# Twelve products instead of six in a step of the dense stream beside the RWKV units

## The chip, the cores and the metric

The kernel runs on one NeuronCore of a Trainium2 chip. The metric is device time in microseconds (us) of one execution. The kernel before took 1853.83 us, the median of 3 runs (1851.74 to 1856.85).

## What is computed

One inference step of a bidirectional hybrid trunk with two layers, float32 in and out, on 128 context tokens and 256 latent tokens (384 columns in all). Layer 0 mixes with a Mamba-2 state-space group (SSD) and an RWKV-7 group side by side, layer 1 with GLA and mLSTM; each layer ends with a squared-ReLU MLP. The change is in layer 0:

```python
def mixer_ab(h, s_ssd, s_rwkv, grid_rows, p):
    proj = h @ p['w_in']
    ssd_in, rw_in = proj[..., :IN_SSD], proj[..., IN_SSD:]
    xbc = silu(short_conv(ssd_in[..., D_SSD:...], ...))
    ...
    rw = rw_in + p['rwkv_mu'] * (token_shift(rw_in) - rw_in)
    ...
    for d in range(2):
        y, s = rwkv7_scan(rh, lw_h[:, :, d], kd, vh, kk, a_h[:, :, d], ...)
    ...
    out = jnp.concatenate([y_ssd, y_rw], axis=-1) @ p['w_out']
```

The RWKV scan runs in chunks of 64 tokens: in each chunk a 64x64 triangular matrix is inverted by doubling, and a state is carried from chunk to chunk.

## The kernel before

Products of the dense projections are split in two for precision: the activations and the weights each have a high and a low half (`h3H`, `h3L`, `wH`, `wL`), and one product of 128 input rows by 128 output columns is three matmuls of 128x384 into one accumulator (`dps`): H by wH, L by wH, H by wL (lines 746 to 749). One output tile has eight such products, 24 matmuls. Weights come in panels of two products; `take` (line 152) has each panel split into wH (ScalarE, line 714) and wL (VectorE, line 715) three panels ahead.

Layer 0 is written as streams of Python generators. `ab_streams` (line 1527) goes through 19 stages; stage s has up to six streams: `chain` (the state recurrence of RWKV unit s-2: `pr`, `pu`, `pd`, `py`), `inv` (the inverse of unit s-1: rounds of `pz`, then `pw2` and `pt2`), `prep0`/`prep1` (operands of unit s), `tail` (norm and gate of a finished head pair: `pm`, `pm2`, `pg`), `ssd1` to `ssd3` (`aux`), and `fill` (the dense products of coming units, of SSD and, in the last stages, of the output projection, with products `mod` for the modulation between them). `run` (line 1584) always steps the stream that is least far along, by the number of steps done over the number expected: `self.steps` holds the numbers, first those written by hand in lines 1533 and 1534, and after a stream has run the number that it had; `PACE` (line 34) scales them. A framework then sets each engine's order from this one, by priority, taking a later instruction where an earlier one isn't ready by its own reckoning.

A step of `fill` is what `dense_cm` (line 728) issues between two `yield`s. Before the change that is a panel, two products (six matmuls), then one step of deferred evacuation work (`step_late`, line 798), then the `yield`:

```python
if self.grain and k % self.grain == self.grain - 1:
    self.step_late()
    yield
```

`self.grain` is 2 (line 2056); `k` counts in the panel. After the last product the accumulator is evacuated and there is one more `yield`. Deferred work is the rest of an evacuation: the SSD convolution (`conv`, line 1006: nine instructions on `cacc` in three parts, then a SiLU) and the token shift of an RWKV column (two instructions, lines 1094 and 1095). In layer 1, `grain` is 2 as well (line 2513). In stages 0 to 15 the dense products have one accumulator bank (`one_acc`), so a new output tile starts when the one before it has been evacuated.

Of the kernel before, what the change touches and what calls it, by code (L numbers as in the profile page):

```python
# [175 lines left out]
class Net:  # L176
# [551 lines left out]
    def dense_cm(self, W, c0, xs, evac, placed=None, blocks=None, ncol=128, width=T, acc=None):  # L728

        if blocks is None:
            n = self.wcfg["nk"] * 128 // ncol
            blocks = [(k, n) for k in range(0, len(xs), n)]

        def steps(dn):
            ps = (self.dacc() if acc is None else acc)[:ncol, :width]
            left = sum(n for _, n in blocks)
            first = acc is None  # L740
            for i, (k0, n) in enumerate(blocks):
                h, lo = dn.take(i)
                for k in range(n):
                    xh, xl = xs[k0 + k]
                    left -= 1
                    self.mm(ps, h[:, k, :], xh, start=first, stop=False)
                    first = False
                    self.mm(ps, h[:, k, :], xl, start=False, stop=False)
                    self.mm(ps, lo[:, k, :], xh, start=False, stop=left == 0 and evac is not None)
                    if self.grain and k % self.grain == self.grain - 1:  # L750
                        self.step_late()
                        yield
            more = evac(ps) if evac is not None else None
            if more is not None and next(more, self) is not self:
                self.late.append(more)
            yield
        return Dense(self, [(W, k0, n, c0, ncol, placed) for k0, n in blocks], steps)
# [769 lines left out]
    def ab_streams(self):  # L1527

        NB = 16
        sh, us, fills = self.sh, self.us, self.fills  # L1530
        st = [dict() for _ in range(NB)]
        py = {}
        self.steps.update({"set": 7, "fill0": 37, "fill1": 24, "fill2": 15, "fill3": 14, "fill14": 16, "fill15": 32, "fill16": 30,
                           "fill17": 29, "ssd1": 11, "ssd2": 6, "ssd3": 9, "prep0": 12, "prep1": 9, "inv": 17, "tail": 3})
        for s in range(NB + 3):
            self.one_acc = s < NB
            self.lpool = LPOOL.get(s, 0)
            if s == 1:

                row = lambda: self.mpool.tile([128, T], F32, tag="nt", name="prow", bufs=2)[:, 0:128]  # L1540
                self.params_tr(self.params_in(range(3, self.params.shape[1] // 128), row, self.nc.sync))
            streams = []
            b = s - 2
            if 0 <= b < NB:
                j, d = divmod(b, 2)
                if d == 0:
                    py[j] = self.psy.tile([128, 512], F32, tag="y", name="py")
                streams.append(("chain", self.rw_chain(j, d, st[b], py[j], sh[j])))
            b = s - 1
            if 0 <= b < NB:  # L1550
                streams.append(("inv", self.seq(self.rw_tokmajor(b % 2, sh[b // 2], st[b]), self.rw_inverse(b % 2, st[b]))))
            b = s
            if b < NB:
                j, d = divmod(b, 2)
                prep = self.rw_prep(j, d, sh[j], st[b])
                if d == 0:
                    streams.append(("prep0", self.seq(self.rw_shared(j, sh[j]), prep)))
                else:
                    streams.append(("prep1", self.seq(prep, self.rw_bonus(j, sh[j]))))
            if s >= 4 and s % 2 == 0 and (s - 4) // 2 < 8:  # L1560
                j = (s - 4) // 2
                streams.insert(0, ("tail", self.rw_tail(j, sh[j], sh[j]["y"])))
            q, g = s % 4, s // 4
            if s < NB and q:
                if q == 1:
                    core = self.ssd_core(g, us[g])
                streams.append(("ssd%d" % q, self.part(core, SSD_PARTS[q])))
            if s == 0:
                streams.append(("set", self.set))
            if fills[s]:  # L1570
                streams.append(("fill%d" % (q if 0 < s < NB - 2 else s), self.pipe(fills[s])))
            self.run(streams)
        return sh[7]["y"]
# [384 lines left out]
    def mixer_ab(self):  # L1958
# [94 lines left out]
        self.AOb, (self.Zb, self.AHb, self.ALb) = bd[:2], bd[2:]  # L2053
        self.rpp = self.pool("rwp", es=eb)
        self.yss = self.sumsq()
        self.grain = 2
        self.drain(self.pipe(self.first[0:4] + [self.flush_late()]))
        self.rw_low()
        self.drain(self.pipe(self.first[4:] + [self.flush_late()]))
# [520 lines left out]
```

## Time and profile before

| | |
|---|---|
| profiled execution, its own time | 1853.32 us |
| its span, first to last instruction | 1851.2 us |
| median of 3 runs | 1853.83 us |
| TensorE (PE) busy | 1765.5 us, 95% of the span |
| VectorE (DVE) busy | 1301.8 us, 70% |
| ScalarE (ACT) busy | 1069.6 us, 58% |
| GpSimd (POOL) busy | 216.6 us, 12% |
| mean granted TensorE clock | 0.98 |

Stages of the program in the span: to 87 us layer 0's norm and first products; 87 to 846 us the streams of `ab_streams`; 846 to 1152 us the MLP of layer 0; 1152 to 1582 us layer 1's mixer; then its MLP. "Busy" is time with an instruction under way. Matmuls overlap: a row's duration is longer than the distance to the next row's start, and it is the distance from start to start that the engine's time is made of. PEclk of 1.00 is the 2.4 GHz level, 0.50 the 1.2 GHz level.

### The profile page before, as it was taken

The page shows a single profiled execution, that of the slowest core. Times are in us where ns is not written, and L with a number is a line of the kernel's source. Part 1 is how long each engine was busy: PE and PEld are TensorE (multiplying, and loading weights), DVE is VectorE, ACT ScalarE, POOL GpSimd, SP SyncE. Part 2 cuts the span into 40 slices and gives each one's busy share as a digit, 9 for nine tenths or more (in the row PEclk, how much of TensorE's full clock was granted, in tenths as well). Part 3 has the DMA queues.
Part 4 walks back from the last instruction along what each step waited for, and adds up shares of the span by engine and source line. Part 5 has one row for each costly group of instructions (what it writes and reads, how often), then busy time and mean ns, then how long its engine had stood idle before and what let it go on. Part 6 is the DMA issues. An engine that isn't in the chain of part 4 may idle for free.

```text
span 1851.2 us, 37384 instructions
## 1 busy us (share of the span) xinstructions
PE 1765.5 (95%) x13661; PEld 1480.9 (80%) x13661; DVE 1301.8 (70%) x2992; ACT 1069.6 (58%) x2688; POOL 216.6 (12%) x270
## 2 busy tenths in 40 slices
PE   7879999999999999999999999899999998999998
PEld 3667767766666677786999998889989897999887
DVE  3698788777878889758766334786786958766434
ACT  3567475746574777646655333777676756755322
POOL 3222111110112011101000000020211212000000
PEclk9889999999999999999999999999999998999999
DMA  8332443333334322345445643333333233344432
GB/s 280 112 88 65 123 133 97 106 87 112 102 105 126 101 65 81 100 119 175 117 124 171 177 146 101 102 91 102 102 94 92 74 108 106 115 125 126 150 134 80
DMA packets 314107, 213.55 MB, mean 115 GB/s; under 512 B 39648, under 2 KB 297494, under 8 KB 313924
## 3 DMA queue, kind: packets, MB, share of 16 engines
q1 hardware_dynamic: 308756, 208.35, 38.6%
q10 hardware_dynamic: 4816, 2.69, 0.5%
q8 instruction: 107, 1.75, 0.4%
q14 instruction: 76, 0.62, 0.1%
q0 software_dynamic: 352, 0.13, 0.0%
HBM read 201.32 MB, written 9.78 MB: 114 GB/s over the span
## 4 chain that ended last, share of the span: by engine, by line
PE 75%; DVE 10%; ACT 8%; DMA 4%; issue 2%; POOL 1%; SPq 0%; DVEq 0%; ACTq 0%; POOLq 0%
PE dps L221 45%; PE o L221 7%; PE ps L221 4%; PE mod L221 3%; PE aux L221 2%; DVE wL L235 2%; PE psc L221 2%; DMA raw<-in_w_mod 2%; PE py L221 1%; PE pt L221 1%; DVE cacc L242 1%; PE pr L221 1%; ACT wH L277 1%; PE pw L221 1%; ACT Zb L277 1%
## 5 line engine op out<-in xcount | busy, mean ns | idle before, releaser
L277 ACT ACTIVATE wH<-raw 128x256 fp32r<-128x256 f32 (+1 forms) x790 | 363.3, 480 | 429.3 <-PE dps L221 309.6
L235 DVE TENSOR_TENSOR wL<-raw,wH 128x256 fp32r<-128x256 f32 (+2 forms) x771 | 398.9, 536 | 243.2 <-ACT wH L277 239.5
L277 ACT ACTIVATE Zb<-pz 64x384 f16<-64x384 f32 x160 | 77.2, 483 | 36.4 <-PE pz L221 34.1
L242 DVE SCALAR_TENSOR_TENSOR cacc<-rows,params,cacc 128x384 f32<-128x384 f32 (+1 forms) x192 | 94.2, 491 | 0.7
L221 PE MATMUL dps<-sH,wH 128*128 128x384 f32 x232 | 85.8, 371 | 4.0 <-DVE m L235 3.5
L221 PE MATMUL dps<-sL,wH 128*128 128x384 f32 x232 | 80.5, 347 | 0.3 <-DVE sL L235 0.2
L221 PE MATMUL dps<-sH,wL 128*128 128x384 f32 x232 | 79.7, 345 | 0.5 <-DVE wL L235 0.5
L221 PE MATMUL dps<-h0H,wH 128*128 128x384 f32 (+1 forms) x147 | 58.9, 401 | 8.2 <-ACT h0H L277 3.5
L235 DVE TENSOR_TENSOR AO<-AHb,rwmask 128x768 f16<-128x768 f16 (+1 forms) x112 | 60.1, 537 | 7.7 <-PE pz L221 6.0
L235 POOL TENSOR_TENSOR BK<-BK,kkk 128x768 f32<-128x768 f32 x16 | 33.8, 2110 | 221.5 <-DVE BK L239 150.5
L221 PE MATMUL mod<-xT,cond 128*32 128x384 f32 (+1 forms) x320 | 55.2, 485 | 3.8 <-DVE Q L235 2.5
L221 PE MATMUL dps<-h6H,wH 128*128 128x384 f32 (+2 forms) x147 | 54.9, 373 | 2.7 <-ACT wH L277 2.7
L221 PE MATMUL dps<-h2H,wH 128*128 128x384 f32 (+1 forms) x147 | 55.6, 378 | 1.4 <-ACT wH L277 1.4
L221 PE MATMUL dps<-h4H,wH 128*128 128x384 f32 (+1 forms) x147 | 54.9, 378 | 2.1 <-ACT h4H L245 2.1
L235 POOL TENSOR_TENSOR gDb<-gb 128x384 f32<-128x384 f32 x28 | 33.2, 1187 | 173.5 <-DVE gb L2230 73.2
L221 PE MATMUL dps<-h1H,wH 128*128 128x384 f32 (+1 forms) x147 | 52.0, 354 | 0.0
L221 PE MATMUL dps<-h6H,wL 128*128 128x384 f32 (+2 forms) x147 | 50.8, 346 | 1.2 <-DVE wL L235 1.2
L221 PE MATMUL dps<-h0H,wL 128*128 128x384 f32 (+1 forms) x147 | 51.7, 351 | 0.0
L221 PE MATMUL dps<-h1H,wL 128*128 128x384 f32 (+1 forms) x147 | 51.6, 351 | 0.0
L221 PE MATMUL dps<-h0L,wH 128*128 128x384 f32 (+1 forms) x147 | 51.5, 356 | 0.0
L221 PE MATMUL dps<-h1L,wH 128*128 128x384 f32 (+1 forms) x147 | 51.3, 355 | 0.0
L221 PE MATMUL dps<-h2H,wL 128*128 128x384 f32 (+1 forms) x147 | 51.1, 348 | 0.0
(1163 smaller groups left out, 5450.0 us busy)
## 6 DMA issues: line engine op xcount, KB each, us to landing
raw<-in_w_mlp_up SPq DMA_DIRECT2D x64, 512.0 KB
raw<-in_w_mlp_down SPq DMA_DIRECT2D x64, 512.0 KB
raw<-in_w_in_ab SPq DMA_DIRECT2D x204, 128.0 KB
xT<-in_w_mod SPq DMA_DIRECT2D x128, 192.0 KB
raw<-in_w_in_cd SPq DMA_DIRECT2D x192, 128.0 KB
raw<-in_w_mod SPq DMA_DIRECT2D x64, 192.0 KB
raw<-in_w_mod SPq DMA_DIRECT2D x32, 256.0 KB
raw<-in_w_out_cd SPq DMA_DIRECT2D x64, 128.0 KB
```

Source lines behind the costliest of these rows:

```text
L221: self.nc.tensor.matmul(out, lhsT, rhs, start=start, stop=stop)
L235: return (eng or self.nc.vector).tensor_tensor(out=out, in0=a, in1=b, op=op)
L242: self.nc.vector.scalar_tensor_tensor(out=out, in0=a, scalar=s, in1=b, op0=op0, op1=op1)
L277: self.nc.scalar.activation(out=out, in_=in_, func=AF.Copy)
```

## The change

`dense_cm` counts products over the whole output tile (`done`) instead of in the panel, and `grain` is 4 in layer 0: a step holds four products, twelve matmuls, and after them two steps of deferred work. An output tile of eight products has two such steps and the evacuation's instead of four and the evacuation's. A tile whose products aren't a multiple of four ends its last step with the last product. The numbers of steps written by hand for the first use of each stream are set anew. In layer 1 `grain` stays 2, and there too each step now calls `step_late` twice.

```diff
         def steps(dn):
             ps = (self.dacc() if acc is None else acc)[:ncol, :width]
             left = sum(n for _, n in blocks)
+            done = 0
             first = acc is None
...
                     self.mm(ps, lo[:, k, :], xh, start=False, stop=left == 0 and evac is not None)
-                    if self.grain and k % self.grain == self.grain - 1:
+                    done += 1
+                    if self.grain and (done % self.grain == 0 or left == 0):
+                        self.step_late()
                         self.step_late()
                         yield
...
-        self.steps.update({"set": 7, "fill0": 37, "fill1": 24, "fill2": 15, "fill3": 14, "fill14": 16, "fill15": 32, "fill16": 30,
-                           "fill17": 29, "ssd1": 11, "ssd2": 6, "ssd3": 9, "prep0": 12, "prep1": 9, "inv": 17, "tail": 3})
+        self.steps.update({"set": 7, "fill0": 18, "fill1": 11, "fill2": 14, "fill3": 16, "fill14": 12, "fill15": 24, "fill16": 22,
+                           "fill17": 34, "ssd1": 11, "ssd2": 6, "ssd3": 9, "prep0": 12, "prep1": 9, "inv": 17, "tail": 3})
...
-        self.grain = 2
+        self.grain = 4
```

What this does to the order of the instructions is seen in the built programs. TensorE in the middle of stage 8, from the last matmul of an inverse round on (`pt_6632` and `pt_6661` are `pt2` of that round; `pu` is the chain's, `dps` the dense products). Before:

```order
L221 MATMUL pt_6632<-Zb,W 64x64
L221 MATMUL dps<-h4H,wH 128x384
L221 MATMUL dps<-h4L,wH 128x384
L221 MATMUL dps<-h4H,wL 128x384
L221 MATMUL dps<-h5H,wH 128x384
L221 MATMUL dps<-h5L,wH 128x384
L221 MATMUL dps<-h5H,wL 128x384
L221 MATMUL pu<-R,WF 64x64 x4
L221 MATMUL dps<-h6H,wH 128x384
```

Now:

```order
L221 MATMUL pt_6661<-Zb,W 64x64
L221 MATMUL pu<-R,WF 64x64 x4
L232 MATMUL pst<-const_base,st 128x64 x2
L232 MATMUL aux<-const_base,B 128x128 x3
L221 MATMUL mod<-xT_6511,cond 32x256
```

The six dense matmuls between `pt2` and `pu` are gone from there; they now stand in one run of twelve further up, before `pw2` of the same round, and the units' matmuls follow one another.

TensorE at the end of the streams, from the last `pr` of the last unit's chain to the first product `mod` behind it (`py` is what the last head pair's tail waits for; `pm`, `pm_13242` and `pg` are that tail). Before:

```order
L221 MATMUL pr<-S,KR 64x64 x2
L221 MATMUL dps<-sH,wH 128x384
L221 MATMUL dps<-sL,wH 128x384
L221 MATMUL pu<-R,WF 64x64 x2
L221 MATMUL dps<-sH,wL 128x384
L221 MATMUL dps<-sH,wH 128x384
L221 MATMUL dps<-sL,wH 128x384
L221 MATMUL py<-Q,UV 64x64
L221 MATMUL dps<-sH,wL 128x384
L221 MATMUL py<-Q,UV 64x64
L221 MATMUL py<-KR,S 64x64 x2
L221 MATMUL mod<-raw,cond 32x384
```

Now:

```order
L221 MATMUL pr<-S,KR 64x64 x2
L221 MATMUL pu<-R,WF 64x64 x2
L221 MATMUL py<-Q,UV 64x64 x2
L221 MATMUL py<-KR,S 64x64 x2
L221 MATMUL mod<-raw,cond 32x384
L221 MATMUL pm<-y,const_base 128x384
L221 MATMUL mod<-raw,cond 32x384 x4
L221 MATMUL pm_13242<-t_13239,const_base 128x384
L221 MATMUL pg<-gdt,g_13235 128x384
L221 MATMUL mod<-raw,cond 32x384 x12
```

The last three links of the chain follow one another with nothing between them, and the twelve dense matmuls that stood before `pm` and between `pm` and `pm_13242` have moved to before the chain's last `pr`.

## Rows read from the trace of the kernel before

**Rows 1.** The profile page: busy time and share of the span by engine.
```profile
PE 1765.5 (95%) x13661; PEld 1480.9 (80%) x13661; DVE 1301.8 (70%) x2992; ACT 1069.6 (58%) x2688; POOL 216.6 (12%) x270
```
**Rows 2.** Stretches, ramp and streams: length, PE, PEld, DVE, ACT, POOL busy, PEclk, DMA share, GB/s.
```profile
87.00:150.00 63.00, 53.50 (x397) 46.55 (x396) 53.96 (x120) 40.96 (x107) 17.05 (x18) 0.87 0.33 85
150.00:846.00 696.00, 673.85 (x7459) 491.51 (x7459) 554.97 (x1388) 429.67 (x1094) 93.73 (x101) 0.99 0.37 105
```
**Rows 3.** Waits of PE from 150 to 846 us: total us, times, longest us.
```profile
PE pw L221 <- ACT Zb L277: 3.1, 5, 1.3
PE pz L221 <- DVE T L235: 3.0, 5, 0.9
PE mod L221 <- DVE Q L235: 2.5, 3, 1.5
...
PE pt L221 <- ACT Zb L277: 1.0, 2, 0.6
...
PE dps L221 <- ACT rows L277: 0.5, 2, 0.3
```
**Rows 4.** Timeline inside the streams: start us, duration us, engine, operation (PEld loads weights).
```profile
303.56 0.33 PE L221 MATMUL dps<-h3L,wH 128*128 128x384 f32 x1
303.56 0.19 PEld L221 LDWEIGHTS dps<-h3H,wL 128*128 128x128 f32 x1
303.74 0.33 PE L221 MATMUL dps<-h3H,wL 128*128 128x384 f32 x1
...
304.67 0.19 PEld L221 LDWEIGHTS dps<-h4L,wH 128*128 128x128 f32 x1
304.67 0.44 PE L221 MATMUL dps<-h4L,wH 128*128 128x384 f32 x1
...
304.95 0.33 PE L221 MATMUL dps<-h4H,wL 128*128 128x384 f32 x1
...
305.47 0.33 PE L221 MATMUL dps<-h5H,wL 128*128 128x384 f32 x1
...
305.74 0.34 PE L221 MATMUL pd<-UV,BKT 128*64 128x64 f32 x4
```
**Rows 5.** Groups of PE matmuls from 150 to 846 us: count, busy us, mean ns, idle before.
```profile
L221 PE MATMUL dps<-h0H,wH 128*128 128x384 f32 x38 | 16.9, 445 | 0.9 <-ACT rows L277 0.5 <-ACT k L245 0.2 <-ACT Z L277 0.2
...
L221 PE MATMUL dps<-h2H,wH 128*128 128x384 f32 x38 | 15.8, 416 | 0.0
...
L221 PE MATMUL dps<-h3L,wH 128*128 128x384 f32 x38 | 12.9, 339 | 0.0
```
**Rows 6.** The convolution's instructions from 150 to 846 us: duration ns min/median/max.
```profile
L242 DVE SCALAR_TENSOR_TENSOR cacc<-rows,params,cacc x96: 393/410/2077, 238.6 to 646.9; 128x192 f32<-128x192 f32 x72, 128x384 f32<-128x384 f32 x24
```
**Rows 7.** Timeline of the streams' end: start us, duration us, engine, operation [idle before].
```profile
834.37 0.33 PE L221 MATMUL pr<-S,KR 64*64 64x64 f32 x4
...
835.49 0.33 PE L221 MATMUL pu<-R,WF 64*64 64x64 f32 x4
...
836.12 0.22 ACT L245 ACTIVATE UV<-pu 64x64 f32<-64x64 f32 x1 [0.21 <-DVE UV L239]
...
837.36 0.33 PE L221 MATMUL py<-KR,S 64*64 64x64 f32 x4
...
837.74 0.49 ACT L277 ACTIVATE y<-py 128x384 f32<-128x384 f32 x1 [1.40 <-PE py L221]
...
839.53 0.81 PE L221 MATMUL pm<-y,const_base 128*128 128x384 f32 x2
...
841.23 0.81 PE L221 MATMUL pm<-t,const_base 128*128 128x384 f32 x2
...
846.73 0.84 PE L221 MATMUL dps<-sH,wlast 128*128 128x384 f32 x2 [1.99 <-ACT sH L277]
```
**Rows 8.** Stretches around two low clocks (columns as in rows 2).
```profile
410.00:420.00 10.00, 10.00 (x51) 5.02 (x48) 5.87 (x18) 1.35 (x3) 0.87 (x1) 0.50 0.32 97
...
455.00:465.00 10.00, 8.60 (x60) 4.03 (x62) 6.38 (x17) 5.19 (x13) 2.43 (x1) 0.83 0.54 165
```

## The prediction

> **What bounds the kernel now.** I read the profile page first [rows 1]: TensorE is busy for 95% of the span. Then busy time by stretch [rows 2]. From 150 to 846 us, where the streams run in steady state, TensorE is busy 673.85 of 696 us, VectorE 554.97, ScalarE 429.67: TensorE is the bound, and 22 us is all that waiting costs there. In the ramp, 87 to 150 us, it is otherwise: VectorE is busy 53.96 of 63 us, TensorE 53.50, at a mean clock of 0.87. Who is waited for [rows 3] shows no single culprit: the largest sum, `pw2` (`pw` in the rows, as `pt2` is `pt`) waiting for the `Zb` copies, is 3.1 us in 5 waits, and `pz` for `T` 3.0 in 5.
>
> A busy engine isn't yet one at its best, so the timeline [rows 4] comes next. Inside a run of dense matmuls the starts are 303.56 and 303.74, 0.18 us apart. The first dense matmul behind a unit's matmuls starts at 304.67 and the next at 304.95: 0.28. The last one before a unit's `pd`, whose array shape is 128*64 instead of 128*128, starts at 305.47 and `pd` at 305.74: 0.27. The weight-load rows beside them say why. Inside the run the load for the matmul of 303.74 starts at 303.56, 0.18 us ahead; behind the unit it starts at 304.67, with its matmul. So each break in a dense run costs TensorE about 0.10 us where the dense stream is entered again, and 0.09 us wherever the shape changes. The groups [rows 5] show it over the whole stretch: the matmul that begins a tile, on `h0H`, has a mean of 445 ns, the one on `h2H`, which begins the second panel, 416, and one in the middle of a panel, `h3L`, 339.
>
> **The change, part by part.** *Order outside the streams.* The built programs agree from the end of layer 0's mixer on, layer 1 included, although `step_late` is called twice there as well. I cost it at nothing; the framework hides it, since a convolution's instructions are a chain on `cacc` and go where VectorE has room.
>
> *Fewer breaks.* In the changed part of the order, dense runs begin 308 times before and 253 times now, 55 fewer. At 0.106 us each, the excess of `h0H` over `h3L` [rows 5], that is 5.8 us. The lower end is 0.077, the excess of `h2H` with its unbroken cases averaged in: 4.2. I take the upper, since each tile begins with an entry and only some of its second panels do. Changes of array shape between neighbours, units among themselves included, fall only from 985 to 954, because a dense run taken out from between two units often leaves two units of different shape side by side. 31 at 0.09 us are 2.8 us; the ends are 0, if the units' own changes come dearer by as much, and 5.0, if all 55 breaks save one. Both terms lie on the bound. I take 5.8 + 2.8 = 8.6 us gained, ends 4.2 and 10.8.
>
> The Trainium skill, "TensorE: Matmul & The Clock Gate", under "Step-by-step: what each phase is for", has TensorE pull the next weight load ahead of matmuls under way, so that it costs no time. Inside a run the trace agrees (0.18 us ahead), at a break it doesn't. By that rule this term would be nothing, and the sum 1856.
>
> *Waits inside the units.* More units' steps now stand between two dense steps, so a pair such as `pz` and the `pw2` that needs its result could lose the work between them. I counted TensorE's own work between the two in either order, at the row's durations. Of 64 such pairs 7 had less than 1.2 us before and 9 now; of 79 from `pt2` to the next `pz` 10 had less than 1.5 and 12 now; `pr` to `pu` under 0.9 us goes from 7 to 11 of 64. So some four more waits of the usual 0.6 us (3.1 in 5, 3.0 in 5) [rows 3]: 2.4 us lost. Against it, where one dense tile hands the accumulator to the next, less than 0.8 us of other work stood 28 times and stands 20 times now; those waits are short (0.5 us in 2) [rows 3], and 8 fewer chances are worth 0.6 at most. Net 1.8 us lost. This is the least certain term: 5 us gained if the waits thin out as they do between tiles, 14 lost if they spread (below).
>
> *Deferred work in pairs.* Two parts of a convolution at once, eight instructions of 0.41 us [rows 6], would hold VectorE's queue 3.3 us if they stood together, and `T`, `W` and `R` of the units behind them. In the orders they don't: instructions on `cacc` stand alone 132 times before and 133 now. Nothing; 16 convolutions at some 0.8 us more, 13 us, if they did, which the order excludes.
>
> *The ramp.* The hand-written numbers now match the streams' real lengths (`fill0` was written as 37 steps and has 28; it is written as 18 and has 18). VectorE, not the dense stream, sets the ramp [rows 2], so I take 0; TensorE's idle time there is 9.5 us, and half of it either way, 5 us, are the ends.
>
> *The end.* Before, the last `py` begins at 837.36, `y` is copied at 837.74, `pm` waits behind dense matmuls until 839.53, the second `pm` until 841.23, and the output's last block starts at 846.73 after an idle 1.99 us [rows 7]. Now `pm` can follow the end of `y`, 838.23, and the second `pm` comes at most the same 1.7 us later, at 839.95: the tail is 1.3 us shorter. But the twelve dense matmuls that hid there, 2.2 us, come ahead of the chain's last `pr`. From that `pr` to the last `py` it now takes 2.99 us with six dense matmuls in between (1.1); without them `pr` to `pu` is some 0.8 (1.12 less two of them), `pu` to the end of `UV` 0.85, the first `py` 0.3: 1.95. So moving those six ahead costs 1.1 and saves 1.0. Sum 1.0 us lost, between 0 and 3.
>
> *Queues.* Weight splits and their loads go with the dense steps, two panels at a time. `dps` waits for no `wH` or `wL` among the waits of this stretch [rows 3], the splits have up to three panels' lead, and a run of twelve takes 2.2 us for its two. Nothing; were that lead gone, some tenths of a microsecond in each run.
>
> The sum: -8.6 + 1.8 + 1.0 = -5.8 us on the profiled execution's 1853.32: 1847.5. The median of the runs stands 0.5 above it, so **1848.0 us**. A difference of 0.3%, 5.6 us, is about what a measurement can tell from none here; the sum lies on that line.
>
> **The rivals.** *Breaks cost nothing, or come back.* Dense runs are only 55 fewer, not half; if a break between two units costs as much as the one saved, only the 5.8 us of entries remain, and waits of 1.8 and the end's 1.0 take half of it back; if the entry's price goes to the units as well, nothing remains. For it: changes of shape hardly fall. Against it: the entry's price is in the mean of 38 tiles [rows 5]. It gives 1853.3 - 3.0 = 1850 to 1853.3 + 2.8 = 1856.
>
> *The clock's low stretches go away.* Behind the longest wait of the stretch, 1.5 us of a `mod` product for `Q` [rows 3], PEclk is 0.50 from 410 to 420 us, the 1.2 GHz level, and 0.83 over another ten [rows 8]. They cost 5.0 and about 1.7 us. The order of these places changes, and if neither wait recurs the time is 1847.5 - 6.7 = 1841. Nothing in the order speaks for that more than for two such places elsewhere.
>
> *Slower: the inverse rounds lose their cover.* The place is `pz`, `pw2`, `pt2` in stages 1 to 16, 144 pairs, each a round trip over ScalarE or VectorE. Twelve of them are waited for now, 7.1 us [rows 3]. The gain of 8.6, less the end's 1.0, is spent when the waits grow by 7.6, that is by some thirteen pairs at 0.6; with 24 more, 14 us, and one more low clock like the one at 455 us, 1.7 us, the time is 1853.3 - 8.6 + 1.0 + 14 + 1.7 = 1861. For it: in stage 1 of the new order `pt`, `pz`, `pw2` and `pt2` follow each other with no dense matmul between. Against it: the counts above. The same skill page, under "HAM oscillation — how this bites in real kernels", says that idle gaps put TensorE back to half clock; the stretch from 410 us agrees, and by it this rival's price is rather too low.
>
> **How the numbers follow.** The forecast has 0.42; as its sum lies on the line, I give 0.30 of that to faster by over 0.3% and 0.12 to within. Breaks that come back 0.24: 0.02 faster, 0.19 within, 0.03 slower. The clock 0.10, faster. The lost cover 0.24: 0.02 within, 0.22 slower. That is 0.42 faster, 0.33 within, 0.25 slower. The range 1836 to 1863 reaches from the low-clock case with the full 11 us of breaks (1839, and some) to the lost cover with both its terms (1861, and some). The forecast's own range is 1842 to 1853.
>
> **What would show it.** Mean durations: `h2H` and `h6H` fall towards 345 ns, while `h0H` and `h4H` stay above 410; TensorE's busy time from 150 us to the end of the streams falls by some 8 us. Waits of PE in that stretch sum to 24 to 28 us, with `pw2` and `pz` first. Layer 1's stretch keeps its 430 us within 1. `pm` follows `y` at once, and the wait before the last output block is 2.5 to 4 us. I am wrong if the sums on `h2H` fall and those of the units' first matmuls rise by as much, if `pw2` and `pz` wait over 14 us, or if the mean clock falls below 0.87 in the ramp or 0.98 in the streams.

## The result, and the profile after

Of four executions of the changed kernel one took 6434.24 us and is left out: the median of the other three is 1872.81 us (1874.26 with it). The kernel before took 1852.78 beside it: a ratio of 1.0103, 95% interval 1.0071 to 1.0135. The change makes the kernel slower by some 19 us, where 1848 was forecast, 6 us faster, in a range that ended at 1863. The profiled execution took 1875.72 us with a span of 1873.9, 22.7 above that of before.

The page of the changed kernel: busy time by engine, and the granted clock of TensorE in 40 slices.

```profile
PE 1777.9 (95%) x13661; PEld 1499.4 (80%) x13661; DVE 1303.0 (70%) x2992; ACT 1073.8 (57%) x2688; POOL 217.8 (12%) x270
...
PEclk9889999999999996999999999999999998999999
```

Against [rows 1], TensorE is busy 12 us longer with the same 13661 matmuls, and one slice of the clock shows a 6. Which stretch lost the time? The streams end with the last `py`, at 837.5 us before and 862.0 now. Busy time by stretch (columns as in [rows 2]), first before, then after:

```profile
150.00:400.00 250.00, 242.84 (x2778) 175.67 (x2779) 204.52 (x510) 158.42 (x406) 35.80 (x33) 1.00 0.37 104
400.00:837.50 437.50, 423.77 (x4644) 311.87 (x4643) 344.03 (x867) 266.62 (x678) 57.93 (x68) 0.98 0.36 102
...
1151.00:1581.00 430.00, 404.52 (x2415) 373.59 (x2408) 333.48 (x747) 295.83 (x835) 64.72 (x85) 0.98 0.35 95
```

```profile
150.00:400.00 250.00, 239.73 (x2722) 174.11 (x2722) 198.78 (x497) 159.72 (x407) 38.08 (x35) 1.00 0.37 106
400.00:862.00 462.00, 443.24 (x4722) 335.86 (x4722) 352.61 (x886) 273.67 (x688) 56.55 (x68) 0.94 0.34 99
...
1175.00:1605.00 430.00, 404.73 (x2420) 373.71 (x2413) 334.83 (x749) 297.65 (x839) 64.89 (x85) 0.98 0.35 95
```

Layer 1 keeps its 430 us. The loss lies in the streams, above all behind 400 us, and there the clock's mean falls from 0.98 to 0.94. The ends of the inverses narrow it down: unit 12 ends 8.4 us later than before, unit 14 20.7. In between the clock stands at half for 30.7 us on end. The same stretch of the program, before and after:

```profile
703.00:734.00 31.00, 29.84 (x359) 24.01 (x358) 28.16 (x70) 21.10 (x57) 4.79 (x4) 1.00 0.32 94
```

```profile
716.00:747.00 31.00, 30.45 (x235) 23.21 (x235) 18.13 (x45) 13.35 (x35) 1.27 (x1) 0.51 0.21 62
```

TensorE is as busy as it was (30.45 us), and gets 235 matmuls done instead of 359. The timeline shows what stands in front of the fall. Before (start, duration, engine, operation, idle before):

```profile
702.24 0.42 PE L221 MATMUL dps<-h6H,wH 128*128 128x384 f32 x1
702.50 0.34 PE L221 MATMUL dps<-h6L,wH 128*128 128x384 f32 x1
703.58 0.34 PE L221 MATMUL pz<-T,AO 128*128 128x64 f16 x6 [0.74 <-DVE T L235]
703.75 0.42 PE L221 MATMUL dps<-h6H,wL 128*128 128x384 f32 x1
704.01 0.34 PE L221 MATMUL dps<-h7H,wH 128*128 128x384 f32 x1
704.19 0.34 PE L221 MATMUL dps<-h7L,wH 128*128 128x384 f32 x1
704.36 0.33 PE L221 MATMUL dps<-h7H,wL 128*128 128x384 f32 x1
704.53 0.27 PE L232 MATMUL pf<-const_base,S 128*64 128x128 f32 x1
```

After:

```profile
712.22 0.35 PE L221 MATMUL pz<-T,AO 128*128 128x64 f16 x6
713.37 0.30 PE L232 MATMUL pf<-const_base,S 128*64 128x128 f32 x1 [0.81 <-DVE S L235]
...
713.79 0.39 PE L221 MATMUL dps<-sH,wH 128*128 128x384 f32 x1
...
715.63 0.33 PE L221 MATMUL pu<-R,WF 64*64 64x64 f32 x4 [0.58 <-DVE R L235]
716.55 0.48 PE L221 MATMUL pz<-T,AO 128*128 128x64 f16 x6 [0.59 <-DVE T L235]
717.02 0.69 PE L221 MATMUL dps<-sL,wH 128*128 128x384 f32 x1
```

Before, the tile's last panel (`h6H` to the second `h7H`) lay around `pz` and ahead of `pf`. Now the step has four products, its last twelve matmuls are through by 707.5 us, and TensorE stands idle for 0.81, 0.58 and 0.59 us ahead of `pf`, `pu` and `pz`, with a single dense matmul between them. The clock falls at 716.0, as the third of these waits begins, and returns at 746.7, when dense runs of eight and six start again. From 720 to 740 us only eleven of the 157 matmuls are dense.

**An account of the streams.** I split the time from 87 us to the last `py` into three, from the trace: *waits* (idle time of over 60 ns ahead of a matmul); *clock* (for the matmuls that started at half clock, their distance to the next start, waits taken out, less the mean distance of the same kind at full clock in the two traces); and the *rest*. What counts as one kind is a choice: others move a clock term by 1 to 3 us, and the rest against it. Before: 30.0 waits, 13.2 clock, 707.3 rest. After: 38.3, 32.0, 704.7. So waits +8.3, clock +18.8, rest -2.6: together 24.5, the shift of the last `py`. What comes behind it is 1.8 us shorter. Time at half clock in that stretch, waits taken out, went from 27.1 to 73.6 us.

**All executions.** A profile is one execution; the record has the span and the mean granted clock of each. Call the span times one less that clock the *lost clock*. Over the 84 executions of the kernel before in the comparisons below it has a mean of 40.1 us, and executions that lose more are longer: by 0.75 us for each us lost (correlation 0.90, where 1 is a straight line). The change has 56.1 in its three, 16.0 more, with a mean span 17.7 us longer. At 0.75 the clock's part is some 12 us of the 18, an estimate; the 18.8 above are of two executions that lost 37.9 and 58.4. So the clock is the larger part of the loss in the mean as well, and a smaller one is not the clock.

### The profile page after: what moved, and what is told of

Its sections match the earlier page's. It is cut to its first block, busy times and chain, and to the rows that moved or that the text cites. A ratio compares the mean times of both kernels' runs of the same rounds, so it can differ in the third digit from the quotient of the medians.

```text
span 1873.9 us, 37393 instructions
## 1 busy us (share of the span) xinstructions
PE 1777.9 (95%) x13661; PEld 1499.4 (80%) x13661; DVE 1303.0 (70%) x2992; ACT 1073.8 (57%) x2688; POOL 217.8 (12%) x270
## 4 chain that ended last, share of the span: by engine, by line
PE 73%; DVE 8%; ACT 4%; issue 2%; DMA 1%; POOL 1%; SPq 0%; DVEq 0%; ACTq 0%; POOLq 0%
PE dps L221 43%; PE o L221 7%; PE ps L221 5%; PE mod L221 2%; PE aux L221 2%; PE py L221 2%; PE psc L221 2%; DVE wL L235 1%; PE pt L221 1%; PE pr L221 1%; PE pw L221 1%; PE ms L221 1%; DVE cacc L242 1%; PE pu L221 1%; PE pd L221 1%
## 5 line engine op out<-in xcount | busy, mean ns | idle before, releaser
L235 DVE TENSOR_TENSOR AO<-AHb,rwmask 128x768 f16<-128x768 f16 (+1 forms) x112 | 55.2, 494 | 6.3 <-PE pz L221 3.9
L221 PE MATMUL mod<-xT,cond 128*32 128x384 f32 (+1 forms) x320 | 48.6, 482 | 4.5 <-DVE Q L235 3.2
L221 PEld LDWEIGHTS dps<-sH,wH 128*128 128x128 f32 x232 | 44.5, 193 | 9.0 <-issue 5.7
```

The costliest lines, as they stand in the source:

```text
L221: self.nc.tensor.matmul(out, lhsT, rhs, start=start, stop=stop)
L235: return (eng or self.nc.vector).tensor_tensor(out=out, in0=a, in1=b, op=op)
```

## The experiments

Theories, formed from this: the **clock theory** (the coarser steps leave places where short waits meet a lack of dense matmuls; the clock falls, and the price is there), against **longer waits** everywhere, the **deferred work** in bursts, and the **written numbers** of the fills. The table holds all runs. Their profiled executions are split as above; the last column has the mean lost clock of all executions of a kernel.

| run | us | ratio to before, 95% | at half clock, us | clock | waits | rest | lost clock |
|---|---|---|---|---|---|---|---|
| before | 1852.78 | | 27.1 | 13.2 | 30.0 | 707.3 | 40.1 |
| change | 1872.81 | 1.0103 (1.0071 to 1.0135) | 73.6 | 32.0 | 38.3 | 704.7 | 56.1 |
| late_twice | 1856.35 | 1.0016 (0.9997 to 1.0034) | 33.4 | 16.5 | 31.6 | 704.0 | 41.0 |
| twelve_then_six | 1856.58 | 1.0001 (0.9983 to 1.0019) | 43.7 | 19.7 | 35.3 | 703.6 | 38.9 |
| six_then_twelve | 1870.41 | 1.0069 (1.0045 to 1.0093) | 71.1 | 33.5 | 33.8 | 705.5 | 52.6 |
| three_per_step | 1886.40 | 1.0168 (1.0151 to 1.0185) | 66.0 | 30.1 | 34.4 | 712.3 | 60.3 |
| change_filled_at_716 | 1864.25 | 1.0053 (1.0035 to 1.0070) | 46.0 | 19.7 | 37.1 | 707.8 | 43.2 |
| six_filled_last_round | 1854.40 | 0.9999 (0.9984 to 1.0014) | 27.8 | 13.0 | 27.7 | 715.0 | 34.5 |
| twelve_late_once | 1869.27 | 1.0092 (1.0059 to 1.0125) | 54.1 | 26.0 | 36.5 | 705.2 | 53.5 |
| twelve_first_weights | 1874.88 | 1.0111 (1.0079 to 1.0142) | 67.2 | 30.6 | 41.7 | 702.2 | 56.7 |
| change_filled_all | 1869.86 | 1.0079 (1.0049 to 1.0109) | 28.2 | 13.5 | 36.6 | 714.2 | 43.9 |
| twelve_six_filled | 1856.92 | 1.0008 (0.9994 to 1.0023) | 20.7 | 10.0 | 33.9 | 711.5 | 32.8 |
| twelve_in_stage_14 | 1861.18 | 1.0034 (1.0019 to 1.0049) | 52.2 | 24.9 | 30.8 | 706.0 | 46.7 |
| six_filled_three_places | 1842.86 | 0.9931 (0.9906 to 0.9955) | 17.6 | 8.6 | 27.8 | 707.8 | 29.0 |
| change_filled_716_647 | 1864.18 | 1.0039 (1.0023 to 1.0056) | 31.4 | 14.5 | 37.8 | 707.3 | 42.3 |
| twelve_six_filled_unit_11 | 1855.77 | 1.0002 (0.9974 to 1.0030) | 44.4 | 19.9 | 34.6 | 704.1 | 40.4 |

Executions of one kernel spread by up to 20 us (before: 1845.5 to 1863.1 over the comparisons), so a profile, which shows one of them, stands for its kernel only in what recurs.

**Deferred work alone (late_twice).** The kernel before, with the change's second call:

```diff
 if self.grain and k % self.grain == self.grain - 1:
     self.step_late()
+    self.step_late()
     yield
```

> Six products a step as before, deferred evacuation work twice at each step: that half of the change alone. Clock theory (what the change lost is TensorE at half clock in stretches that hold no dense work): the order on TensorE stays that of before, so 1849 to 1858 us and half-clock time between 87 us and the end of the streams near the 31 us of before (over 87 us, without the low stretch at 79). Deferred-work theory (bursts of evacuation work hold up the unit's casts and masks, and so the waits): 1863 us or more, with waits of TensorE in the streams up by 8 us.

No difference that can be told; the interval ends at 0.34%, 6 us, so the doubled deferred work alone is not the cause. But its profile holds a fall that the profile of before doesn't, at 288.6 us for 17.1 us. Before, in the stretch of the same place, and late_twice:

```profile
288.60:305.70 17.10, 17.10 (x242) 13.68 (x242) 15.61 (x39) 11.43 (x29) 3.63 (x3) 1.00 0.20 52
```

```profile
288.60:305.70 17.10, 17.10 (x167) 13.70 (x168) 10.01 (x26) 7.30 (x17) 0.61 (x1) 0.50 0.17 44
```

Ahead of it stand these waits in late_twice, at the last `pt2` of unit 3; before has them as 0.63, 0.32 and 0.18 us:

```profile
286.14 0.19 PE L221 MATMUL pt<-Zb,W 64*64 64x64 f16 x1 [0.63 <-ACT Zb L277]
286.65 0.35 PE L221 MATMUL pt<-Zb,W 64*64 64x64 f16 x11 [0.32 <-ACT Zb L277]
...
287.67 0.93 PE L221 MATMUL psc<-KR,BK 64*128 64x128 f32 x6 [0.45 <-DVE BK L235]
```

**Where the steps are coarse (twelve_then_six, six_then_twelve).** In the loop over stages, the first:

```diff
+            if s == 13:
+                self.grain = 2
+                self.steps.update({"fill1": 16, "fill14": 16, "fill15": 32, "fill16": 30, "fill17": 29})
```

(below 13 the steps of the change, from 13 on those of before); the second the other way round, with the change's numbers from stage 13 on.

> The change in stages 0 to 12, six products a step from stage 13 on (from about 640 us). The change lost some 6 us until 690 us and 15 between 690 and 790, where the clock stood at half for 30.7 us on end. Clock theory: with finer steps there the long low stretch goes, 1855 to 1863 us. Waits theory (every unit waits longer, the clock is by the way): 13 of 16 units keep the cost, 1867 to 1872 us.

> The converse: six products a step in stages 0 to 12, twelve from stage 13 on. Clock theory: the stretch of 716 to 747 us has the steps of the change, so 1864 to 1871 us, with 20 us or more at half clock after 640 us. Waits theory: 3 of 16 units pay, 1854 to 1858 us.

Thirteen stages of coarse steps cost nothing that can be measured, though waits (35.3) and half-clock time (43.7 us) are above before in that profile (over its ten executions the lost clock, 38.9, is not); six stages from 13 on cost 0.7%. Both halves together stay under the change's 1.0%, within the intervals. The stretch from 714.4 us is the change's once more, with as few matmuls:

```profile
714.40:745.10 30.70, 30.70 (x233) 23.76 (x234) 16.90 (x41) 12.83 (x32) 1.26 (x1) 0.50 0.22 64
```

That is the clock theory's outcome in both. Until about 640 us, six_then_twelve has before's order on TensorE, instruction for instruction, and yet fell at 291 us for 17.1 us, behind the same 0.63, 0.32 and 0.18 us of idle that the profile of before passed at full clock.

**The converse, in one stage (twelve_in_stage_14).** Before, with `self.grain = 4 if s == 14 else 2`, `"fill14": 12`, and the change's way of stepping where `grain` is 4.

> The kernel before with twelve products a step in stage 14 alone (and its first weight 12), four dense runs fewer in all: the converse of the fill at 716. Clock theory: the six products that stood between the waits of pf, pu and pz move away, the clock falls for 25 to 31 us near 705 us as it did with the change, 1863 to 1869 us. Breaks and waits as priced: four breaks fewer and under 1 us of waits, 1853 to 1856 us.

```profile
714.50:731.60 17.10, 17.10 (x160) 13.57 (x160) 11.14 (x26) 6.69 (x18) 1.27 (x1) 0.50 0.24 70
```

Four dense runs fewer cost 0.34% (0.19 to 0.49), some 6 us: the fall comes, behind idle of 0.88, 0.58 and 0.59 us at `pf`, `pu` and `pz`, but lasts 17.1 us, and the time stays 2 us under the range expected. Over its ten executions the lost clock is 6.6 us more than before's. At 291 us this execution fell for 6.8 us: three executions of the same order up to there (before and these two) show 0, 17.1 and 6.8 us at half clock.

**The place filled (change_filled_at_716).** The cause undone without touching the steps: the change, with products of constants in the idle time, written into the bank of the waiting product, which overwrites them.

```diff
+    def hold(self, p, n):
+        for _ in range(n):
+            self.mm(p[:, :T], self.i128h, self.rwmask[:, 0:T])
...
                 pf = self.psc("pf")
+                self.hold(pf, 5 if self.stage == 14 else 0)
...
             pu = self.psc("pu")
+            self.hold(pu, 3 if self.stage == 14 and s == 2 else 0)
```

and three ahead of the third `pz` of that stage.

> The change, and in stage 14 alone eleven small extra products (constants times constants, 128 x 384 in half precision, written into the bank of the product that waits and overwritten by it): five ahead of pf, three ahead of pu, three ahead of pz, where TensorE stood idle for 0.81, 0.58 and 0.59 us before the clock fell at 716 us. They are 11 x 0.17 = 1.9 us of work, in 2.0 us of idle. Clock theory: the half-clock stretch of 30.7 us does not come, so some 12 us less than the change, 1860 to 1866 us, with the three waits shorter in the profile. Waits theory, or that the thin stretch of itself costs the time: 1872 to 1876 us.

The timeline of the place (only rows with extra products and with waits), and the stretch:

```profile
711.71 0.65 PE L221 MATMUL pf<-rwmask,i128h 128*128 128x384 f16 x3
712.20 0.65 PE L221 MATMUL pz<-rwmask,i128h 128*128 128x384 f16 x3
...
713.82 0.30 PE L237 MATMUL pf<-const_base,S 128*64 128x128 f32 x1 [0.47 <-DVE S L240]
...
716.08 0.65 PE L221 MATMUL pu<-rwmask,i128h 128*128 128x384 f16 x3 [0.34 <-DVE R L240]
```

```profile
716.00:747.00 31.00, 30.64 (x347) 23.87 (x347) 27.21 (x68) 19.49 (x53) 3.91 (x3) 1.00 0.32 91
```

Eleven added matmuls make the change some 9 us faster (1.0053 against 1.0103), and 347 matmuls instead of 235 fit into the 31 us. The lost clock is 12.9 us less than the change's, which at 0.75 is 9.7 us, the whole gain. Outside 711 to 748 us the order is the change's; inside, some 70 of 282 matmuls change place too. But up to 717.8 us no dense matmul comes forward (the change has one at 713.79), so what stands ahead of the fall differs by the filler and the order of small matmuls, and this fall's price is shown: about half of the loss. Filler ends idle time and adds large products at once; which of the two holds the clock the runs don't separate. This execution fell at 646.9 us for 17.1 us, behind the last `pt2` of unit 11.

**More places of the change filled (change_filled_all, change_filled_716_647).** Four more extra products, ahead of the last `pt2` of every inverse from stage 2 on (60 in all), or of unit 11's alone.

> The change with the eleven extra products of stage 14 and four ahead of the last pt of each inverse: 71 in all. With the eleven alone the profiled execution still fell to half clock at 647 us for 17 us, right behind 0.49 and 0.32 us of idle at such a pt. Clock theory: that stretch goes too, some 7 us under the 1864 us of the eleven alone, 1855 to 1861 us; what then still lies above before is the added waits. If the fills cost their work: 1866 to 1872 us.

> The change with the eleven extra products of stage 14 and four ahead of the last pt of unit 11 alone, after whose 0.49 and 0.32 us of idle the clock fell for 17 us with the eleven (for 7 us without). Clock theory: 4 to 7 us under the 1864 us of the eleven, 1857 to 1861 us, and what still lies above before is waits and lesser falls. If the clock falls elsewhere instead: 1863 to 1867 us.

Neither got below the first fill. With all 60 the clock's price is that of before (13.5), but the rest rises to 714.2: most of their 10 us of work found no idle time to lie in, as the second outcome had it. With unit 11's four, the profiled execution has no fall at 647 or 716:

```profile
640.00:670.00 30.00, 28.46 (x390) 22.73 (x389) 27.86 (x71) 18.64 (x45) 6.28 (x5) 1.00 0.22 57
```

It took 1860.03 us, within the range expected; the median, 1864.18, is not (executions from 1854.5 to 1869.2), the second outcome: the granted clock is 0.982 in the fastest of the ten executions and 0.973 in the slowest. That profile tells most of the second part of the loss: with the clock's price at 14.5, near before's 13.2, it lies 6.7 us above before's profiled execution, and its waits are 7.8 us more. By this account the second part is waits; no run takes away the waits alone.

**Coarse steps before stage 13, filled (twelve_six_filled, twelve_six_filled_unit_11).**

> Twelve products a step to stage 12, six from stage 13 on, and four extra products ahead of the last pt of each inverse. Without them its profiled execution fell at 644 us for 24 us, right behind 0.63 and 0.32 us of idle at a last pt, at a cost of 10 to 12 us. Clock theory: that fall goes, 1846 to 1852 us, under the kernel before. If the fall only moves to another wait: 1853 to 1858 us.

> Twelve products a step to stage 12, six from stage 13 on, with four extra products ahead of the last pt of unit 11 alone (its profiled execution without them: 24 us at half clock from 644 us). Clock theory: 8 to 10 us under the 1856.6 us without them, 1846 to 1849 us: the coarse steps of stages 0 to 12 would then be worth about what their breaks save. If 56 of the 60 extra products of the run with all last rounds filled were not what kept that run at 1857 us: 1854 to 1858 us again.

Both miss the clock theory's range and lie in the other. The first held the clock (20.7 us at half) and gained nothing: its rest is 4.2 us and its waits are 3.9 us above those of before, which takes what the clock gave. The second didn't hold it: its profile falls at 647.8 us again for 20.5 us. Whether coarse steps in the early stages would pay with the clock held at no cost stays open; nothing here says so.

**Finer steps (three_per_step).** `self.grain = 1`, numbers to match.

> Three products a step (one row block of weights), first weights of the fills set to match. The dense runs go from 296 to 363 by the program. Breaks cost as the prediction priced them: 67 at 0.106 us, 7 us more than before. Clock theory: shorter stretches without dense work, half-clock time from 100 us to the end of the streams under 15 us, which gives back 5 to 8 us: 1848 to 1856 us together. If only breaks count: 1858 to 1862 us. If waits fall with finer steps too, under 1848 us.

Missed by 30 us. Finer steps didn't keep the clock up: it fell at 292.8 us, behind the 0.63 and 0.32 us of idle of unit 3's last `pt2`, met 2.2 us more of idle, and stayed down for 24 us, in which eight of 206 matmuls are dense:

```profile
292.80:316.70 23.90, 22.06 (x206) 17.37 (x207) 15.15 (x40) 10.17 (x24) 2.19 (x4) 0.50 0.14 37
```

Of 29.9 us more in the span, 16.9 are clock, 4.4 waits, 5.0 rest and the others lie behind the streams. The 5.0 are near the 67 added breaks at 0.106 us (7.1), as far as the split can tell.

**Deferred work once (twelve_late_once) and first weights (twelve_first_weights).** The change with one `step_late()` a step; and with `"fill0": 24, "fill1": 16`.

> The change with the deferred evacuation work once a step instead of twice, so half as often as before per product. Deferred-work theory: bursts are smaller, waits fall, 1860 to 1868 us. Clock theory: the place of the dense work hardly moves, 1868 to 1880 us. A third outcome: deferred work comes so late that accumulators or dependent steps wait, 1880 us or more.

> The change with the first weights of the fills of stages 0 and 1 at 24 and 16 instead of 18 and 11, which are as far above the true counts as those of before were (there 37 for 28 steps and 24 for 17). Numbers theory (the change also lets the first two fills come later): the ramp is faster, 1866 to 1871 us, and units 0 and 1 end some 3 us sooner. Otherwise 1872 to 1877 us.

In the first, part of what it computes differs from the change, presumably because some deferred parts come behind steps that read their result; it has the same instructions in another order. 1869.27 is not apart from the change (the intervals overlap), and its profile has 19.5 us less at half clock: inconclusive between the theories. The second is no faster than the change: the first weights aren't the cause.

**Before, filled (six_filled_last_round, six_filled_three_places).** The first has four extra products ahead of every last `pt2`; the second sixteen in all: six ahead of the fourth `pw2` in stages 7 and 8, four ahead of the last `pt2` in stage 4.

> The kernel before, with four such extra products ahead of the last pt of each inverse (0.63 and 0.32 us of idle in the profile of before at 287 us, after which one execution of the same order kept the clock and two let it fall for 17 us): 60 extra products, 10 us of work if none of it fell into idle time, 0 if all. Clock theory: no fall near 290 us in any execution, which saves half of some 8 us on the mean of executions; 1846 to 1856 us, and a narrower spread. If the fills cost their full work: 1860 us or more.

> The kernel before with sixteen extra products at the three places of its profile where idle time led to a fall or nearly did: six ahead of the fourth pw of units 6 and 7 (1.50 and 1.27 us of idle, falls at 410 and 458 us of 10 and 3 us), four ahead of the last pt of unit 3. 2.7 us of work, most of it in idle time. Clock theory: the low 13.6 us after 400 us go, about 6 us less: 1846 to 1851 us. If other waits let the clock fall instead in most executions, or the idle ahead of mod stays: 1852 to 1857 us.

The first lies in the clock theory's range but gains nothing: its profile has no fall near 290 us and its executions lose 5.6 us less clock, but the rest rises by 7.7, most of its 60 x 0.17 = 10 us of work. The second beats both kernels, at 1842.86 us, 0.9931 (0.9906 to 0.9955), 11 us under before. Its profile around the three places, against [rows 8]:

```profile
282.00:300.00 18.00, 17.51 (x249) 13.66 (x249) 15.44 (x43) 10.87 (x26) 0.61 (x1) 1.00 0.27 77
405.00:420.00 15.00, 13.40 (x127) 7.96 (x126) 11.18 (x29) 5.92 (x19) 3.35 (x4) 0.89 0.37 113
455.00:465.00 10.00, 9.71 (x75) 5.64 (x70) 6.91 (x18) 3.29 (x8) 0.00 (x0) 1.00 0.53 163
```

The fall at 458 us is gone and that at 410 shortened from 10.2 to 3.4 us, though its wait stays: a `mod` still waits 1.60 us for `Q`, and five of the six extra products come behind it. In this profiled execution the streams are 6.3 us shorter than in before's: 4.6 clock and 2.2 waits less, 0.5 rest more. It is the slowest of the four; the others took 1842.2 to 1843.1. Over all four the lost clock is 11.1 us less than before's, at 0.75 some 8 of the 12.0 us by which the mean span is shorter. Which places gave the rest of that the profiles don't show: the fall near 290 us, which before's order takes in some executions, is a likely one, though no profile of before itself has it. The extra products also change the order between 408 and 503 us, so part of the gain may be the order's.

## Why the prediction was wrong

*Fewer breaks, 8.6 us.* The mechanism was right, the size not. The dense groups after, to set against [rows 5]:

```profile
L221 PE MATMUL dps<-h0H,wH 128*128 128x384 f32 x38 | 17.1, 450 | 2.6 <-ACT rows L277 2.2 <-ACT k L245 0.4
...
L221 PE MATMUL dps<-h4H,wH 128*128 128x384 f32 x38 | 16.1, 424 | 0.0
...
L221 PE MATMUL dps<-h6H,wH 128*128 128x384 f32 x39 | 13.6, 349 | 0.0
...
L221 PE MATMUL dps<-h2H,wH 128*128 128x384 f32 x38 | 13.5, 354 | 0.0
```

Before:

```profile
L221 PE MATMUL dps<-h6H,wH 128*128 128x384 f32 x38 | 16.3, 430 | 0.0
```

`h2H` fell from 416 to 354 ns and `h6H` from 430 to 349, while `h0H` and `h4H` stayed above 410, as foretold: over 38 of each that is 5.4 us, near the 5.8 of the entries. But the whole rest fell by 2.6 us only, and before and late_twice, nearly the same order, differ by 3.3 there (707.3 and 704.0). So at most some 3 us reached the sum, as the first rival had it; where the others went, and the 2.8 for changes of array shape, can't be seen.

*Waits inside the units, 1.8 us.* They grew by 8.3. The counting of pairs was right where it counted: `pw` and `pz` wait hardly more than in [rows 3]. It left out the other places where a step of dense work had been the cover (waits from 150 to 870 us):

```profile
PE pw L221 <- ACT Zb L277: 3.5, 5, 2.1
...
PE pz L221 <- DVE T L235: 2.9, 5, 0.7
PE dps L221 <- ACT rows L277: 2.2, 3, 0.9
PE py L221 <- DVE UV L239: 2.1, 4, 0.9
PE pf L232 <- DVE S L235: 1.6, 3, 0.8
```

Before:

```profile
PE py L221 <- DVE UV L239: 0.4, 1, 0.4
PE pf L232 <- DVE S L235: 0.3, 1, 0.3
```

`py` and `pf` are the chain, which the count took up at `pr` and `pu` alone. The first matmul of a tile, 2.2 us against 0.5 [rows 3], is the handover of the accumulator, for which I had taken a gain of 0.6.

*The clock, 0 us.* This is the step that failed. The prediction saw half-clock stretches behind waits [rows 8], priced them at 5.0 and 1.7 us, and put the term at nothing, because "nothing in the order speaks for that more than for two such places elsewhere". The order did speak: it takes the six dense matmuls of 702 to 704 us out from between the waits of `pf`, `pu` and `pz`, in front of a stretch with few dense matmuls of its own. In place of nothing the clock cost 18.8 us more in the profiled execution and some 12 in the mean of executions, and eleven extra matmuls at that one place took 9 us of the loss back. The mean clock, 0.96 from 150 to 870 us and 0.86 in the ramp, is under the 0.98 and 0.87 that the prediction named as its refutation. The Trainium skill, "TensorE: Matmul & The Clock Gate", under "A second HAM failure mode: psum-queue depth-cycling", tells of frequent micro-idles between groups of matmuls that send the clock back and forth. Here waits of 0.81 and 0.58 us stand ahead of the fall and one of 0.59 begins with it, for data and not for banks.

*The end, +1.0 us.* Right but for one item. From the last `pr` to the last `py` it now takes 1.82 us (1.95 foretold, 2.99 before), `pm` follows `y`, and the second `pm` comes 1.63 us behind it (1.7 foretold).

```profile
860.11 0.33 PE L221 MATMUL pr<-S,KR 64*64 64x64 f32 x4
860.77 0.33 PE L221 MATMUL pu<-R,WF 64*64 64x64 f32 x4 [0.33 <-DVE R L235]
...
861.93 0.33 PE L221 MATMUL py<-KR,S 64*64 64x64 f32 x4
...
862.95 0.91 PE L221 MATMUL pm<-y,const_base 128*128 128x384 f32 x2
...
864.58 0.91 PE L221 MATMUL pm<-t,const_base 128*128 128x384 f32 x2
```

The wait of 2.5 to 4 us ahead of the output's last block didn't come: products `mod` fill it.

*Terms at nothing.* Deferred work (late_twice, within 6 us), the numbers (twelve_first_weights) and layer 1 (its 430 us) were rightly put there.

*The rivals.* The slower one had the sign and the mechanism, lost cover, and gave 1861. It placed it at `pz` and `pw2`, which didn't change, with 14 us of waits (8.3) and one more low clock of 1.7 us (18.8). That the breaks' gain largely vanishes, as the first rival had it, came true as well.

## What to carry to other kernels

Work that stands between dependent steps covers their latency, and in this kernel it also held TensorE's clock: six dense matmuls gone from between three waits, 2.0 us in all, and 30.7 us at half clock followed. When work is coalesced, look in the new order for places where two or three short waits come together ahead of a stretch of small products, and price a fall there by the length of that stretch, not by the waits. A few matmuls on constants, in the idle time of just those places, were worth more than the same filler everywhere (sixteen took the kernel before to 0.9931, sixty to 0.9999). One profile doesn't show all the falls of a kernel.

## What was not expected of the hardware

A single long wait need not do it: the longest of the changed kernel, 2.13 us ahead of a `pw2` at 279.48 us, left the clock at 1.00, with products `mod` and `pg` around it.

```profile
276.00:284.00 8.00, 5.87 (x53) 2.25 (x51) 6.91 (x16) 3.77 (x11) 0.31 (x1) 1.00 0.65 185
```

In three other kernels a fall of 3.4 us stood behind the same 2.13 us (twelve_first_weights, change_filled_all, twelve_six_filled), in four more none did. The same order with the same waits fell in some executions and not in others. And half clock didn't quite double the time: 73.6 us at half clock cost 32.0, or 43%. Of the dense matmuls around the return of the clock in the changed kernel, two at half clock start at 745.37 and 745.69 us, 0.32 apart, two at full clock at 747.25 and 747.42, 0.17 apart. The Trainium skill, "TensorE: Matmul & The Clock Gate", under "HAM oscillation — how this bites in real kernels", reckons half of the throttled time as lost; by that the estimate would be 36.8 us.
